# Gated DeltaNet preparation: key norms and write gates move from the VectorE products into the exponent of the decays

## The chip, the cores and the metric

The kernel runs on one core of a Trainium2 chip. The metric is device time in microseconds (us) of one execution. TensorE (PE in the rows) multiplies matrices, VectorE (DVE) and GpSimd (POOL) do elementwise work, ScalarE (ACT) does activations, and DMA queues are fed from SP, ACT and POOL.

## The reference, cut to what matters

One layer of a hybrid block over 256 context and 1024 latent tokens. Four of its heads are a bidirectional gated DeltaNet. For every chunk of tokens and both directions it needs

```
q = l2_normalize(q) * HEAD_DIM ** -0.5;  k = l2_normalize(k)
decay = where(i >= j, exp(G[i] - G[j]), 0)          # G: cumulative log-decay of the chunk
kb = k * beta
A  = where(i > j, (kb @ k.T) * decay, 0)            # then (A + I) is inverted
qk = (q @ k.T) * decay
```

The kernel keeps raw keys and queries in DRAM and puts their norms in later. With `nk` the squared norm of key j (plus epsilon), a column of the matrix and of the scores needs the factor beta/nk beside the decay. The rest of the layer is retention in four more heads, an output projection and a SwiGLU.

## The kernel before

The chunk is 128 tokens, so there are TT = 10 tiles of tokens (tiles 0 and 1 are context), and every tile has two directions d: 20 units. Projections for keys and queries (`conv_block`, with a short convolution on VectorE at L586) and token-major projections (`token_major`, PE tile `tm`) surround the preparation `pre(t)` (L660 to L702). A library scheduler with a timing model sets each engine's order inside one program; TensorE work of later stages is put between the small steps. Each engine then runs its own list strictly in order.

`pre(t)` does for one tile:

- PE: `kk` (L665, keys by keys), for latent tiles also `qt` (L670, transposes whose squares ACT sums at L672) and `kq` (L675). These and the transposes `vT` of the values share three PSUM banks ("pb").
- per direction: `gw` is a broadcast row of G fetched by DMA (L678). POOL subtracts the column's own G with four 128-wide instructions, one a head (L683, `e<-gw,nG`), and masks with one 512-wide affine select (L685). ACT takes the exponential, 512 wide (L687). VectorE multiplies `kk` by the column factor `ab` = beta/nk and by `e`, four 128-wide instructions (L695, into `ut`); for latent tiles it does the same with `kq` (L697, into `sp`). ACT also takes exp of `gw` in place (L700), and POOL multiplies it by the query tile (L701). DMAs take `ut` and `sp` to DRAM.

The tiles `gw`, `e`, `ut` and `sp` have two buffers each. `BATCH` groups the tiles in three sets; after a set, `invert(b)` (L708) does a 62-instruction chain on VectorE, its results go to DRAM as `xd`, and `merge(b)` (L756) fetches them back as `U` and `t` and multiplies 32-wide blocks on PE (tile `m`, L771 to L798). `ab` is made in `kstat` (L609), where it is also a factor of `kds`. `nG` is -G (L553), and `softplus` (L141) gives the log-decays from `av`.

Of the kernel before, what the change touches and what calls it, by code (L numbers as in the profile page):

```python
# [8 lines left out]
F32 = mybir.dt.float32  # L9
F32R = mybir.dt.float32r  # L10
I32 = mybir.dt.int32
AF = mybir.ActivationFunctionType
ALU = mybir.AluOpType
# [4 lines left out]
P = 128  # L18
# [5 lines left out]
TT = NTOK // P  # L24
LT = NLAT // P
H = 4
# [3 lines left out]
NEG = -200.0  # L30
GROUPS = ["rv", "rk", "rq", "rg", "z"]
# [6 lines left out]
def build(nc, tc, ap, dbg=None, stop=None, marks=None):  # L38
    root = ExitStack()
    V, S, G, T, SY = nc.vector, nc.scalar, nc.gpsimd, nc.tensor, nc.sync  # L40
# [30 lines left out]
    def bc(a, shape, axis):  # L71
        return a.unsqueeze(axis).to_broadcast(shape)
# [68 lines left out]
    def softplus(pl, x, n, tag):  # L141

        a = pl.tile([P, n], F32, tag=tag + "a", name=tag + "a")
        s = pl.tile([P, n], F32, tag=tag + "s", name=tag + "s")
        q = pl.tile([P, n], F32, tag=tag + "q", name=tag + "q")
# [12 lines left out]
        return s  # L158

    banks(pa=3, pb=3, pc=2)  # L160
    try:
# [35 lines left out]
        xts, raws, small = {}, {}, {}  # L197
# [327 lines left out]
        def c8(t, d):  # L525
# [6 lines left out]
        av = AB.tile([P, TT * 8], F32, tag="av", name="av")  # L532
        V.tensor_tensor(av.rearrange("p (t c) -> p t c", c=8), xa[:, :, 0:8],
                        bc(small["dtb"], [P, TT, 8], 1), ALU.add)
        S.activation(nA, small["alog"], AF.Exp)
        V.tensor_scalar(nA, nA, -1.0, None, ALU.mult)
        sp = softplus(AB, av, TT * 8, "sp")
# [95 lines left out]
        nkf = nk.rearrange("p t h -> p (t h)")  # L633
        sv = rsqrt(GS, nkf, TT * H, "sv")
# [25 lines left out]
        def pre(t):  # L660
# [15 lines left out]
            for d in range(2):  # L676
# [3 lines left out]
                e = GP.tile([P, H, P], F32, tag="e", name="e", bufs=2)  # L680
                for h in range(H):
                    col = t * 8 + d * 4 + h
                    G.tensor_scalar(e[:, h, :], gw[:, h, :], sm["nG"][:, col:col + 1], 1.0, ALU.add, ALU.mult)  # L683
                sg = 1 if d == 0 else -1
                G.affine_select(out=e, in_=e, compare_op=ALU.is_ge, fill=NEG, base=0,  # L685
                                pattern=[[0, H], [sg, P]], channel_multiplier=-sg)
                S.activation(e, e, AF.Exp)  # L687
# [3 lines left out]
                for h in range(H):  # L691
                    col = t * 8 + d * 4 + h
                    hs = slice(h * P, (h + 1) * P)
                    abc_ = sm["ab"][:, col:col + 1]
                    V.scalar_tensor_tensor(ut[:, h, :], pk[:, hs], abc_, e[:, h, :], ALU.mult, ALU.mult)  # L695
                    if t >= 2:
                        V.scalar_tensor_tensor(sp[:, 0, h, :], pq[:, hs], abc_, e[:, h, :], ALU.mult, ALU.mult)  # L697
# [917 lines left out]
```

## Time and profile before

| | us |
|---|---|
| median of 3 timed runs | 1484.18 (1483.59 to 1484.78) |
| profiled execution, its own time | 1486.29 |
| its span, first to last instruction | 1484.5 |
| TensorE busy in the span | 1406.9 (95%) |
| VectorE / ScalarE / GpSimd busy | 974.2 / 604.9 / 628.4 |
| mean granted TensorE clock, of full speed | 0.977 |

TensorE is busy in nearly all of the span, so the places to look at are those where it is not, or where it runs at the lower clock. The preparation lies between 281 and 372 us; the last two of the ten tiles follow up to 436 us, and the three merges lie between 423 and 537 us.

### The profile page before, as it was taken

What the parts mean: (1) busy time and instruction counts of PE and PEld (TensorE: products, weight loads), DVE (VectorE), ACT (ScalarE), POOL (GpSimd) and SP (SyncE); (2) the same over time, 40 slices, a digit from 0 to 9 for tenths busy, and PEclk for the clock granted to TensorE, in tenths of its full rate; (3) what the DMA queues carried; (4) which work ended last, traced back from release to release, by engine and by line L of the source; (5) the groups of instructions that cost most, each with busy time, mean ns of one, the idle gap of its engine ahead of it and who ended that gap; (6) DMA issues with size and microseconds to landing.
All of it is one profiled execution on the core that took longest, in us unless ns stands there. A gap on an engine that the chain in (4) does not pass through costs nothing.

```text
span 1484.5 us, 24226 instructions
## 1 busy us (share of the span) xinstructions
PE 1406.9 (95%) x8919; PEld 1206.4 (81%) x8919; DVE 974.2 (66%) x1938; ACT 604.9 (41%) x1268; POOL 628.4 (42%) x581
## 2 busy tenths in 40 slices
PE   7999999987988899999799899999999999999997
PEld 2798888976878899999688688777888888788886
DVE  6566788269868345689767876656555555657486
ACT  5543564375541121245534533323333333444454
POOL 0120011377124343234134689899555553335321
PEclk9999999998999899999899999999999999999999
DMA  8536686578597755996633265765222242776863
GB/s 321 208 99 212 188 250 202 165 233 273 175 266 204 248 186 205 414 361 221 204 114 114 85 207 215 258 243 183 106 107 107 106 144 79 237 278 190 308 204 114
DMA packets 176567, 298.16 MB, mean 201 GB/s; under 512 B 43496, under 2 KB 93880, under 8 KB 172096
## 3 DMA queue, kind: packets, MB, share of 16 engines
q1 hardware_dynamic: 124896, 253.17, 49.5%
q10 hardware_dynamic: 49072, 35.83, 7.7%
q0 software_dynamic: 2480, 7.60, 1.4%
q8 instruction: 70, 1.15, 0.3%
q14 instruction: 49, 0.40, 0.1%
HBM read 206.60 MB, written 89.96 MB: 200 GB/s over the span
## 4 chain that ended last, share of the span: by engine, by line
PE 42%; POOL 4%; DMA 2%; DVE 1%; issue 1%; ACT 0%; SPq 0%; POOLq 0%; ACTq 0%; DVEq 0%
PE ffn L1306 7%; PE ffn L1305 7%; PE ffn L1304 7%; PE fo L1432 4%; PE fo L1430 4%; PE fo L1431 4%; PE op L1163 2%; PE op L1164 2%; PE op L1165 2%; DMA wd<-tw 1%; POOL ws L1277 1%; POOL tw L1358 1%; POOL tw L1357 1%; DVE wlo L315 1%; POOL tw L1359 0%
## 5 line engine op out<-in xcount | busy, mean ns | idle before, releaser
L341 PE MATMUL tm<-whi,hhi 128*128 128x256 f32 (+1 forms) x704 | 201.1, 289 | 5.6 <-ACT xa L354 1.6
L342 PE MATMUL tm<-wlo,hhi 128*128 128x256 f32 (+1 forms) x704 | 201.3, 288 | 0.6 <-DVE wlo L315 0.6
L343 PE MATMUL tm<-whi,hlo 128*128 128x256 f32 (+1 forms) x704 | 199.2, 287 | 0.0
L341 PEld LDWEIGHTS tm<-whi,hhi 128*128 128x128 f32 x704 | 134.0, 191 | 10.0 <-ACT xa L354 2.4
L1304 PE MATMUL ffn<-t,whi 128*128 128x512 f32 x352 | 137.0, 390 | 2.0 <-ACT whi L314 2.0
L1306 PE MATMUL ffn<-t,wlo 128*128 128x512 f32 x352 | 137.1, 390 | 1.5 <-DVE wlo L315 1.5
L1305 PE MATMUL ffn<-t,whi 128*128 128x512 f32 x352 | 137.0, 389 | 0.0
L314 ACT ACTIVATE whi<-wraw 128x512 fp32r<-128x512 f32 (+2 forms) x98 | 75.2, 771 | 151.4 <-PE ffn L1305 80.5
L342 PEld LDWEIGHTS tm<-wlo,hhi 128*128 128x128 f32 x704 | 134.6, 191 | 1.8 <-DVE wlo L315 1.1
L343 PEld LDWEIGHTS tm<-whi,hlo 128*128 128x128 f32 x704 | 134.1, 192 | 1.8 <-issue 0.9
L314 ACT ACTIVATE whi<-ws 128x512 fp32r<-128x512 f32 x88 | 55.6, 632 | 175.4 <-PE ffn L1305 121.6
L315 DVE TENSOR_TENSOR wlo<-ws,whi 128x512 fp32r<-128x512 f32 x88 | 94.3, 1073 | 47.7 <-ACT whi L314 47.5
L1430 PE MATMUL fo<-whi,ahi 128*128 128x512 f32 x308 | 119.3, 390 | 1.3 <-ACT ahi L314 1.3
L1431 PE MATMUL fo<-wlo,ahi 128*128 128x512 f32 x308 | 119.9, 389 | 0.0
L1432 PE MATMUL fo<-whi,alo 128*128 128x512 f32 x308 | 119.0, 390 | 0.0
L315 DVE TENSOR_TENSOR wlo<-wraw,whi 128x512 fp32r<-128x512 f32 (+2 forms) x92 | 100.3, 1092 | 25.0 <-ACT whi L314 25.0
L1304 PE MATMUL ffn<-b,whi 128*128 128x512 f32 x264 | 103.9, 393 | 4.1 <-ACT whi L314 4.1
L1306 PE MATMUL ffn<-b,wlo 128*128 128x512 f32 x264 | 103.9, 394 | 1.1 <-DVE wlo L315 1.1
L1305 PE MATMUL ffn<-b,whi 128*128 128x512 f32 x264 | 103.8, 393 | 0.0
L576 PE MATMUL b<-hhi,whi 128*128 128x512 f32 (+1 forms) x256 | 96.3, 376 | 1.5 <-ACT y L580 1.5
L578 PE MATMUL b<-hhi,wlo 128*128 128x512 f32 (+1 forms) x256 | 95.2, 372 | 0.0
L577 PE MATMUL b<-hlo,whi 128*128 128x512 f32 (+1 forms) x256 | 94.9, 371 | 0.0
(427 smaller groups left out, 3494.6 us busy)
## 6 DMA issues: line engine op xcount, KB each, us to landing
adaw<-ada_w SPq DMA_DIRECT2D x48, 512.0 KB, 4.6
pk<-sd SPq DMA_DIRECT2D x16, 1536.0 KB, 10.1
wraw<-wfi SPq DMA_DIRECT2D x44, 512.0 KB, 4.0
ar<-ad SPq DMA_DIRECT2D x33, 512.0 KB, 4.7
w<-wfo SPq DMA_DIRECT2D x22, 512.0 KB, 4.6
wd<-tw SPq DMA_DIRECT2D x11, 1024.0 KB, 4.8
ad<-act SPq DMA_DIRECT2D x20, 512.0 KB, 3.0
raw<-wd SPq DMA_DIRECT2D x20, 512.0 KB, 4.9
```

The costliest lines, as they stand in the source:

```text
L314: S.activation(hi, raw, AF.Copy)
L315: e.tensor_tensor(lo, raw, hi.bitcast(F32), ALU.subtract)
L341: T.matmul(o, hhi[:, k, tsl], whi[:, k % 4, :], start=(k == 0), stop=False)
L342: T.matmul(o, hhi[:, k, tsl], wlo[:, k % 4, :], start=False, stop=False)
L343: T.matmul(o, hlo[:, k, tsl], whi[:, k % 4, :], start=False, stop=(k == KT - 1))
L576: T.matmul(o, whi[:, k, :], hh, start=(k == 0), stop=False)
L1304: T.matmul(o, whi[:, k, :], xhi(xn, slice(0, 4), k), start=(first and k == 0), stop=False, **kw)
L1305: T.matmul(o, whi[:, k, :], xlo(xn, slice(0, 4), k), start=False, stop=False, **kw)
L1306: T.matmul(o, wlo[:, k, :], xhi(xn, slice(0, 4), k), start=False, stop=(k == 3), **kw)
L1430: T.matmul(po[g][i], ahi[:, ts], whi, start=(j == 0 and not kw), stop=False, **kw)
L1431: T.matmul(po[g][i], ahi[:, ts], wlo, start=False, stop=False, **kw)
L1432: T.matmul(po[g][i], alo[:, ts], whi, start=False, stop=(j == FH - 1), **kw)
```

## The change

- `softplus` now runs on two halves at once: the decay's argument and minus the gate's argument, so that its second half is -log(beta). `lnb` is the negated second half.
- A new function `log` takes log(nk) for all 40 columns by exponent and mantissa, 22 VectorE instructions; two more put log(beta) - log(nk) into `nG`.
- In `pre(t)` the four POOL subtractions are gone; the affine select reads `gw` and writes `e`, with -1e30 outside the mask. The exponential becomes four 128-wide ACT instructions, one a head, each with its column of `nG` as bias. The four `ut` products become one 512-wide product of `kk` and `e`, and likewise the `sp` products.

```diff
-        sp = softplus(AB, av, TT * 8, "sp")
+        sp = softplus(AB, av.rearrange("p a n -> p (a n)"), 2 * TT * 8, "sp")
+        lnb = GS.tile([P, TT, 2, H], F32, tag="lnb", name="lnb")
+        V.tensor_scalar(lnb.rearrange("p t d h -> p (t d h)"), sp[:, TT * 8:], -1.0, None, ALU.mult)
+        sp = sp[:, :TT * 8]
...
+        lnk = log(GS, nkf, TT * H, "ln").rearrange("p (t h) -> p t h", h=H)
+        nG4 = sm["nG"].rearrange("p (t d h) -> p t d h", d=2, h=H)
+        V.tensor_tensor(lnb, lnb, bc(lnk, [P, TT, 2, H], 2), ALU.subtract)
+        V.tensor_tensor(nG4, nG4, lnb, ALU.add)
...
                 e = GP.tile([P, H, P], F32, tag="e", name="e", bufs=2)
+                sg = 1 if d == 0 else -1
+                G.affine_select(out=e, in_=gw, compare_op=ALU.is_ge, fill=FAR, base=0,
+                                pattern=[[0, H], [sg, P]], channel_multiplier=-sg)
                 for h in range(H):
                     col = t * 8 + d * 4 + h
-                    G.tensor_scalar(e[:, h, :], gw[:, h, :], sm["nG"][:, col:col + 1], 1.0, ALU.add, ALU.mult)
-                sg = 1 if d == 0 else -1
-                G.affine_select(out=e, in_=e, compare_op=ALU.is_ge, fill=NEG, base=0,
-                                pattern=[[0, H], [sg, P]], channel_multiplier=-sg)
-                S.activation(e, e, AF.Exp)
+                    S.activation(e[:, h, :], e[:, h, :], AF.Exp, bias=sm["nG"][:, col:col + 1])
...
-                for h in range(H):
-                    col = t * 8 + d * 4 + h
-                    hs = slice(h * P, (h + 1) * P)
-                    abc_ = sm["ab"][:, col:col + 1]
-                    V.scalar_tensor_tensor(ut[:, h, :], pk[:, hs], abc_, e[:, h, :], ALU.mult, ALU.mult)
-                    if t >= 2:
-                        V.scalar_tensor_tensor(sp[:, 0, h, :], pq[:, hs], abc_, e[:, h, :], ALU.mult, ALU.mult)
+                V.tensor_tensor(ut.rearrange("p h i -> p (h i)"), pk, e.rearrange("p h i -> p (h i)"), ALU.mult)
+                if t >= 2:
+                    V.tensor_tensor(sp[:, 0].rearrange("p h i -> p (h i)"), pq, e.rearrange("p h i -> p (h i)"), ALU.mult)
```

The scheduler's order changes between the softplus and the first steps of the scan, and is the same before and after that stretch, apart from line numbers. Lines of the changed kernel are 30 to 35 higher in this part: its exponential of `e` is L726, the `gw` exponential L735, the affine select L722, the two products L730 and L732, the silu of the convolution L624.

On ACT, early in the preparation, around the silu of one convolution block (`u` and `y` are the two copies out of a convolution's PSUM bank), the order before is

```order
L589 ACTIVATE y<-y 128x1280
L579 ACTIVATE u<-b_3767 128x512
L580 ACTIVATE y<-b_3767,cw 128x512
L700 ACT_TABLE_LOAD
L700 ACTIVATE gw<-gw 128x512
L687 ACTIVATE e<-e 128x512
L314 ACTIVATE whi<-wraw 128x8x128
L700 ACTIVATE gw<-gw 128x512
```

and around the same silu after the change

```order
L615 ACTIVATE y<-b_3699,cw 128x512
L624 ACT_TABLE_LOAD
L624 ACTIVATE y<-y 128x1280
L726 ACT_TABLE_LOAD
L726 ACTIVATE e<-e,nG 128x128 x4
L712 ACTIVATE qt,nq<-qt 128x128
L735 ACTIVATE gw<-gw 128x512
L712 ACTIVATE qt,nq<-qt 128x128 x2
L726 ACTIVATE e<-e,nG 128x128 x3
```

A unit has four short exponentials where it had one long one, and its `gw` exponential now stands behind them. ACT has 22 table loads in either program.

On SP, the queue that feeds the first merge (`t` and `U` are fetched for it, `rope` is a table loaded into the space of the value tiles), the order before is

```order
L834 DMA rope<-rope 128x1280
L702 DMA sd<-sp 128x1024
L752 DMA t_4269<-xd_3091 32x32x32 x2
L702 DMA sd<-sp 128x1024
L678 DMA gw<-grow_d 128x512
L752 DMA t_4269<-xd_3091 32x32x32 x2
L751 DMA U_4267<-xd_3091 32x32x32 x2
L698 DMA un_2862<-ut 128x512
L751 DMA U_4267<-xd_3091 32x32x32 x2
```

and after the change

```order
L737 DMA sd<-sp 128x1024 x2
L718 DMA gw<-grow_d 128x512
L869 DMA rope<-rope 128x1280
L787 DMA t_4173<-xd_3079 32x32x32 x4
L733 DMA un_2894<-ut 128x512
L786 DMA U_4171<-xd_3079 32x32x32 x4
```

The fetches of `t` stand together directly behind the `rope` load; the store of `sp` and the `gw` fetch that stood between them stand ahead of it.

## Rows read from the trace of the kernel before

**Rows 1.** Stretches: length; busy PE, PEld, DVE, ACT, POOL; clock; DMA share; GB/s

```profile
281.00:372.00 91.00, 77.50 (x428) 66.89 (x426) 71.24 (x177) 55.80 (x124) 65.14 (x94) 0.89 0.73 236
372.00:500.00 128.00, 109.48 (x1545) 105.49 (x1546) 92.95 (x240) 45.02 (x99) 34.23 (x55) 0.93 0.75 218
860.00:950.00 90.00, 90.00 (x399) 74.53 (x398) 62.89 (x63) 25.94 (x44) 81.23 (x53) 1.00 0.63 224
```

**Rows 2.** PE's waits, 281 to 372 us: us in total, times, longest

```profile
PE vT L820 <- DVE ut L695: 3.4, 1, 3.4
PE kk L665 <- ACT qt L672: 3.3, 1, 3.3
PE qt L670 <- DVE ut L695: 3.0, 1, 3.0
PE b L576 <- ACT y L580: 1.5, 3, 0.9
PE vT L820 <- ACT qt L672: 1.1, 1, 1.1
```

**Rows 3.** ACT's waits in the same stretch

```profile
ACT gw L700 <- POOL e L683: 20.9, 8, 5.9
ACT e L687 <- POOL e L685: 4.1, 5, 1.4
```

**Rows 4.** Stretches of 5 us in it, columns as in Rows 1

```profile
330.00:335.00 5.00, 5.00 (x29) 5.00 (x29) 3.88 (x11) 4.64 (x11) 3.23 (x6) 0.60 1.00 373
360.00:365.00 5.00, 4.36 (x14) 3.27 (x15) 4.33 (x11) 3.12 (x8) 3.21 (x5) 0.50 0.95 296
```

**Rows 5.** Groups by line, 281 to 372 us: busy us, mean ns, idle before

```profile
L695 DVE SCALAR_TENSOR_TENSOR ut<-kk,ab,e 128x128 f32<-128x128 f32 x64 | 19.1, 341 | 32.1 <-ACT e L687 32.1
L697 DVE SCALAR_TENSOR_TENSOR sp<-kq,ab,e 128x128 f32<-128x128 f32 x48 | 14.6, 340 | 0.0
L683 POOL TENSOR_SCALAR e<-gw,nG 128x128 f32<-128x128 f32 x64 | 31.9, 515 | 23.0 <-DVE ut L695 15.9 <-DVE tmp L730 3.8 <-DMA gw<-grow_d 1.7
L687 ACT ACTIVATE e<-e 128x512 f32<-128x512 f32 x18 | 11.1, 626 | 4.3 <-POOL e L685 4.1
```

**Rows 6.** Single lines and a timeline row: nearest forms of the new instructions

```profile
L977 ACT ACTIVATE XI<-dist,lgs x8: 388/391/393, 608.7 to 610.7; 128x128 f32<-128x128 f32 x8
L1036 DVE TENSOR_TENSOR pm<-rP,M x8: 661/682/699, 643.7 to 714.9; 128x512 f32<-128x512 f32 x8
360.71 1.14 ACT L823 ACTIVATE vt<-vT,svy 128x128 f32<-128x128 f32 x4 [3.03 <-DMA sd<-vt]
L113 DVE TENSOR_TENSOR svu<-svy x3: 192/192/199, 230.4 to 235.9; 128x40 f32<-128x40 f32 x3
```

**Rows 7.** ACT's timeline: start us, us, instruction, idle before it

```profile
323.48 0.63 ACT L700 ACTIVATE gw<-gw 128x512 f32<-128x512 f32 x1 [1.88 <-POOL e L683]
325.22 1.28 ACT L589 ACT_TABLE_LOAD   x1
327.69 0.26 ACT L672 ACTIVATE qt<-qt 128x128 f32<-128x128 f32 x1
```

**Rows 8.** PE's waits, 415 to 500 us, and SP's timeline there

```profile
PE m L778 <- DMA U<-xd: 4.0, 2, 3.0
PE m L771 <- DMA t<-xd: 3.9, 3, 2.6
...
419.15 3.41 SPq L702 DMA_DIRECT2D sd<-sp  x1
423.09 1.63 SPq L752 DMA_DIRECT2D t<-xd  x2
```

**Rows 9.** PE's timeline: two token-major matmuls in a row

```profile
254.80 0.28 PE L341 MATMUL tm<-whi,hhi 128*128 128x256 f32 x1
254.92 0.28 PE L342 MATMUL tm<-wlo,hhi 128*128 128x256 f32 x1
```

**Rows 10.** VectorE's timeline: the first product of the preparation

```profile
283.16 2.16 DVE L695 SCALAR_TENSOR_TENSOR ut<-kk,ab,e 128x128 f32<-128x128 f32 x8 [23.70 <-ACT e L687]
```

More of the change, by code (lines that the diff above doesn't have):

```diff
@@ L30 @@
 NEG = -200.0
+FAR = -1e30
 GROUPS = ["rv", "rk", "rq", "rg", "z"]
@@ L158, in softplus, with log @@
         return s
+    def log(pl, x, n, tag):
+        i = pl.tile([P, n], I32, tag=tag + "i", name=tag + "i")
+        m = pl.tile([P, n], F32, tag=tag + "m", name=tag + "m")
+        e = pl.tile([P, n], F32, tag=tag + "e", name=tag + "e")
+        f = pl.tile([P, n], F32, tag=tag + "f", name=tag + "f")
+        V.tensor_scalar(i, x.bitcast(I32), 23, None, ALU.logical_shift_right)
+        V.tensor_copy(e, i)
+        V.tensor_scalar(m.bitcast(I32), x.bitcast(I32), 0x7FFFFF, 0x3F800000, ALU.bitwise_and, ALU.bitwise_or)
+        V.tensor_scalar(f, m, 1.4142135, None, ALU.is_gt)
+        V.scalar_tensor_tensor(e, e, -127.0, f, ALU.add, ALU.add)
+        V.tensor_scalar(f, f, -0.5, 1.0, ALU.mult, ALU.add)
+        V.tensor_tensor(m, m, f, ALU.mult)
+        V.tensor_scalar(f, m, 1.0, None, ALU.add)
+        V.reciprocal(f, f)
+        V.scalar_tensor_tensor(f, m, -1.0, f, ALU.add, ALU.mult)
+        q = m
+        V.tensor_tensor(q, f, f, ALU.mult)
+        a = pl.tile([P, n], F32, tag=tag + "a", name=tag + "a")
+        V.tensor_scalar(a, q, 1.0 / 15.0, None, ALU.mult)
+        for k in (13, 11, 9, 7, 5, 3):
+            V.scalar_tensor_tensor(a, a, 1.0 / k, q, ALU.add, ALU.mult)
+        V.scalar_tensor_tensor(a, a, 1.0, f, ALU.add, ALU.mult)
+        V.tensor_scalar(f, e, 0.6931471805599453 - 0.693359375, None, ALU.mult)
+        V.scalar_tensor_tensor(a, a, 2.0, f, ALU.mult, ALU.add)
+        V.scalar_tensor_tensor(a, e, 0.693359375, a, ALU.mult, ALU.add)
+        return a
     banks(pa=3, pb=3, pc=2)
@@ L531, in build @@
         CHUNKS = [(0, 256), (256, 512), (768, 512)]
-        av = AB.tile([P, TT * 8], F32, tag="av", name="av")
-        V.tensor_tensor(av.rearrange("p (t c) -> p t c", c=8), xa[:, :, 0:8],
-                        bc(small["dtb"], [P, TT, 8], 1), ALU.add)
+        av = AB.tile([P, 2, TT * 8], F32, tag="av", name="av")
+        av3 = av.rearrange("p a (t c) -> p a t c", c=8)
+        V.tensor_tensor(av3[:, 0], xa[:, :, 0:8], bc(small["dtb"], [P, TT, 8], 1), ALU.add)
+        V.tensor_scalar(av3[:, 1], xa[:, :, 8:16], -1.0, None, ALU.mult)
         S.activation(nA, small["alog"], AF.Exp)
         V.tensor_scalar(nA, nA, -1.0, None, ALU.mult)
-        sp = softplus(AB, av, TT * 8, "sp")
+        sp = softplus(AB, av.rearrange("p a n -> p (a n)"), 2 * TT * 8, "sp")
+        lnb = GS.tile([P, TT, 2, H], F32, tag="lnb", name="lnb")
+        V.tensor_scalar(lnb.rearrange("p t d h -> p (t d h)"), sp[:, TT * 8:], -1.0, None, ALU.mult)
+        sp = sp[:, :TT * 8]
         V.tensor_tensor(sm["g"].rearrange("p (t c) -> p t c", c=8), sp.rearrange("p (t c) -> p t c", c=8),
```

## The prediction

> **What bounds the kernel now.** I read the busy time by stretch first. In the feed-forward part TensorE is busy in all of the 90 us shown and runs at full clock [rows 1]: nothing that the change touches can be worth anything there, and the order of instructions there is unchanged. In the preparation, 281 to 372 us, TensorE is busy for only 77.5 of 91 us, and its granted clock is 0.89 [rows 1]. So 13.5 us are idle. The clock adds to that: a granted 0.60 in a stretch of 5 us with TensorE fully busy costs 2.0 us, and 0.50 with 4.36 us busy costs 2.2 us [rows 4]. (1 - 0.89) x 91 = 10.0 us is the most that the low clock can cost in the stage; part of it falls on idle time, and I put 7 us on work. The stage thus loses about 20.5 us. From 372 to 500 us another 18.5 us are idle at a clock of 0.93 [rows 1]; this is where the merges are.
>
> Then I read TensorE's waits in that stage, because they say which engine would have to be earlier. VectorE's `ut` products release PSUM banks late, for 3.4 + 3.0 = 6.4 us; ACT is late for 3.3 us and 1.1 us with the squares of `qt`, and for 1.5 us with the convolution's copies, 5.9 us together [rows 2]. Both engines have a cause further back. VectorE waits for the exponential of `e` for 32.1 us in the stage [rows 5], of which 23.7 us stand ahead of its first product and cost nothing [rows 10], so 8.4 us inside. ACT, busy for 55.8 of 91 us [rows 1], waits for POOL: its in-place exponential of `gw` must wait until POOL's four subtractions have read `gw`, 20.9 us in 8 waits, and 4.1 us for the affine select [rows 3]. POOL's subtractions hold 31.9 us of its time in the stage, 64 at a mean of 515 ns [rows 5]. The loop is therefore POOL to ACT to VectorE to the PSUM bank to TensorE, and POOL's subtractions are its longest member.
>
> **The change, part by part.** *POOL.* The 64 subtractions in the stage go, 31.9 us of 65.1 us busy [rows 1, 5]. What stays is the affine select. ACT's wait of 20.9 us was for the removed instruction; what is late next for the `gw` exponential is the affine select, for which ACT waited 4.1 us in all [rows 3].
>
> *VectorE.* The stage's 64 + 48 products, 19.1 + 14.6 = 33.7 us [rows 5], become 16 + 12 = 28 products, 512 wide, with one operand in PSUM. The nearest row has the same form: 0.682 us [rows 6]. That is 28 x 0.682 = 19.1 us, a saving of 14.6 us of VectorE's 71.2 us in the stage [rows 1].
>
> *ACT.* Of 18 exponentials in the stage at 0.626 us [rows 5] each becomes four. No row has an exponential with a per-partition bias. The nearest are eight 128-wide exponentials with a per-partition scale, started within 2.0 us and 0.39 us long, so 1.2 us for four, and a packet of four scaled copies at 1.14 us [rows 6]. I take 1.2 us, since that is the same function on SBUF. The addition is 18 x (1.2 - 0.626) = 10.3 us; ACT then needs 55.8 + 10.3 = 66.1 us in a stage in which TensorE's work at full clock is 77.5 - 7 = 70.5 us. A rule speaks against the change here: the Trainium skill, "ScalarE: Activation LUTs", in the section on what ACT_TABLE_LOAD costs, gives an activation with a pointer bias a fixed part of about 280 ns, of which about 93 ns overlap with a neighbour. By that rule, as an estimate, four would take 1.27 us and the addition in the stage would be 11.6 us, close to the rows' price; no row shows the bias form itself.
>
> *Logarithm and gate.* 24 small VectorE instructions at 0.19 us, from a 40-wide row [rows 6], are 4.6 us, plus some 2 us for the doubled softplus by the same row. They lie ahead of 283 us, where VectorE idles for 23.7 us before its first product [rows 10]. I cost them at nothing; without that cover they would delay the first exponentials by at most 6.6 us, and TensorE has convolution work there.
>
> *What leaves TensorE's path.* The `ut` waits, 6.4 us [rows 2]: the products are shorter, their input comes earlier; I take all of it off. The clock: the low stretches lie in the part of the stage in which TensorE waits, so with fewer waits I take off 5 of the 7 us (bounds 0 and 7). The waits for ACT, 5.9 us: the order of squares, table loads and silu on ACT is of the same kind as before. The wait of 3.3 us for `qt` came from a 1.88 us wait for POOL followed by a table load and a silu between two squares [rows 7]; the first part goes, but four exponentials stand among the squares now. I leave all of it standing. Bounds: it goes (-5.9), or ACT's additional 10.3 us comes on top (+10.3). A value nearer to the first bound is right because up to 25.0 us of ACT's waits for POOL [rows 3] fall away against 10.3 us of added work.
>
> *Merges.* In the first merge TensorE waits 3.9 us for `t` [rows 8]. SP had spent 3.41 us on a store of `sp` ahead of the second pair of fetches, issued at 423.09 us [rows 8]; now the four fetches follow the `rope` load directly. I take 2 us off; bounds 0 and -3.9. Between the first merge's last product and the next one's second stage there were 128 + 38 token-major matmuls and are 115 + 34 + 3, 14 fewer at 0.12 us [rows 9]: the wait of 4.0 us for `U` [rows 8], at the end of a chain of stores and fetches with a length of its own, grows by 1.7 us.
>
> The sum: -6.4 - 5 - 2 + 1.7 = -11.7 us. From the profiled execution's 1486.3 us that is 1474.6 us; the median of the runs shown is 2.1 us lower, so I say 1472.5, rounded to 1473 us.
>
> **The rivals.** *More than that.* If ACT's late squares were all POOL's doing, the stage would lose only a few us: -20.5, with -3.9 and +1.7 in the merges, -22.7 us, 1461.5 us. For it: the waits for POOL are the largest in the stage [rows 3]. Against: ACT would be busy for 66.1 of about 71 us, in order, with waits on TensorE itself.
>
> *The gain is given back (no change).* The stage ends earlier, but the merges hang on a chain of VectorE's inversion, stores and fetches, and the values' copies, which have one buffer and wait for the store of the one before (3.03 us in one instance [rows 6]). If the stage's 11.4 us only become waits at the first merge, the sum is 0 to -3: 1481 to 1484 us. Against: TensorE has token-major work to put there, and the inversion on VectorE speeds up with the rest.
>
> *ACT becomes the bound (slower).* ACT serves the squares, the convolution's copies and the value copies for which TensorE already waits. If ACT's waits for POOL turn into waits for something else of the same length (VectorE's release of `e`, or `gw`'s fetch), the 10.3 us pass through to TensorE, while the 6.4 us of `ut` waits, which follow ACT, stay: 1484.2 + 10.3 = 1494.5 us. ACT is idle for 91 - 55.8 = 35.2 us of the stage [rows 1]; at an unchanged length the added work leaves 24.9 us. So this case begins where ACT's waits after the change come to more than 24.9 us in the stage. A milder form, with half of it, gives 1489 us.
>
> *The change doesn't do what it says*, by more table loads: ACT has 22 in either program, so I give that no chance of its own.
>
> **How the numbers follow.** A measurement here can tell 0.2%, 3 us, from no change. Forecast, -5 to -17 us: 0.60; more: 0.14; given back: 0.16; slower by ACT: 0.10. Of the forecast's own range all lies beyond -3 us, of the given-back case nearly all within. Faster 0.74, same 0.16, slower 0.10. The forecast's range is 1467 to 1479; down to 1462 takes in most of the first rival, and up to 1485 the second; the third is left out.
>
> **What would show it.** The preparation should take 78 to 82 us instead of 91, with TensorE's waits on the `ut` product nearly gone and its waits on `qt` and on the convolution's copies still there. ACT's wait for POOL should fall from 25 us to under 8, POOL's busy time in the stage to about 33 us. The products should cost 0.66 to 0.70 us, four exponentials 1.1 to 1.3 us. The first merge should wait less for `t`, the second somewhat more for `U`. After the merges all stretches should have their old lengths. I am wrong if ACT is busy to over 90% of a stage that did not shorten, or if the first merge waits longer by what the stage gained.

## The result, and the profile after

The changed kernel takes 1489.57 us, median of 16 runs (1485.42 to 1496.22), against 1484.86 us before: a ratio of 1.0032, 95% interval 1.0020 to 1.0043. It is 0.3% slower; 1473 us was forecast, with 1485 as the upper end. Repeated on another chip it took 1490.54 us, ratio 1.0039 (1.0025 to 1.0053). The first profile is of the fastest of its 16 runs (1485.42 us, span 1483.3 us) and so shows less than the whole loss. The second, of the repetition, is of an execution of 1490.93 us, span 1488.8 us, close to its median. Both are used below, and a reading is kept where they agree.

The single operations became what was forecast. Groups by line after the change, 281 to 372 us (line, engine, operation, tiles, shapes, count, busy us, mean ns, then idle before them and what ended it):

```profile
L730 DVE TENSOR_TENSOR ut<-kk,e 128x512 f32<-128x512 f32 x16 | 10.9, 687 | 36.0 <-PE kk L705 22.1 <-ACT e L726 8.4 <-POOL e L722 3.4
L732 DVE TENSOR_TENSOR sp<-kq,e 128x512 f32<-128x512 f32 x12 | 8.1, 678 | 0.0
L726 ACT ACTIVATE e<-e,nG 128x128 f32<-128x128 f32 x72 | 23.1, 390 | 16.8 <-POOL e L722 16.3 <-ACT vt L858 0.5
L722 POOL TENSOR_SCALAR_AFFINE_SELECT e<-gw 128x512 f32<-128x512 f32 x16 | 13.8, 865 | 32.7 <-DMA gw<-grow_d 14.8 <-DVE ut L730 13.4 <-DVE y L621 4.2
```

VectorE's 112 products of 33.7 us [rows 5] are 28 of 19.0 us, the 64 subtractions on POOL are gone, and the exponentials cost 23.1 us where they cost 11.1.

The stages show where it goes wrong. Stretches of the kernel before, from 372 us, and of the first profile after, from 281 us (length; busy PE, PEld, DVE, ACT, POOL; granted clock; DMA share; GB/s):

```profile
372.00:420.00 48.00, 44.98 (x377) 44.24 (x378) 36.43 (x88) 24.87 (x70) 7.36 (x9) 1.00 0.66 196
420.00:500.00 80.00, 64.50 (x1170) 61.24 (x1169) 56.52 (x154) 20.15 (x30) 26.86 (x46) 0.89 0.80 232
500.00:540.00 40.00, 40.00 (x589) 38.57 (x588) 13.44 (x39) 8.70 (x16) 18.32 (x35) 1.00 0.59 193
```

```profile
281.00:372.00 91.00, 77.78 (x445) 68.36 (x444) 70.39 (x104) 68.06 (x180) 34.74 (x30) 0.91 0.77 238
372.00:420.00 48.00, 40.39 (x330) 39.78 (x329) 32.54 (x75) 21.43 (x65) 4.89 (x5) 0.93 0.70 214
420.00:500.00 80.00, 68.63 (x1202) 65.37 (x1201) 53.19 (x131) 22.88 (x38) 26.19 (x43) 0.89 0.73 199
500.00:540.00 40.00, 38.23 (x571) 36.72 (x569) 13.47 (x38) 6.62 (x12) 15.97 (x31) 1.00 0.66 224
```

In the preparation TensorE issues more matmuls than before in the same 91 us (445 against 428 [rows 1]), at a clock of 0.91 instead of 0.89. In the next 48 us it loses them: 7.6 us idle instead of 3.0, 330 matmuls instead of 377, and a clock of 0.93 instead of 1.00. From 420 to 540 us, where the merges are, it idles for 13.1 us instead of 15.5 (12.8 in the second profile). From 281 to 540 us that makes 32.0 us of idle time before, and 34.0 and 35.5 after.

The same in milestones. First and last start of the convolution's matmuls (b) and of the token-major matmuls (tm), which fill TensorE's gaps until the merges are over; before, then after the change in the second profile:

```profile
L576 PE MATMUL b<-hhi,whi x256: 276/392/796, 112.0 to 370.5; 128*128 128x512 f32 x96, 128*128 128x256 f32 x32
L341 PE MATMUL tm<-whi,hhi x704: 274/281/582, 38.2 to 581.2; 128*128 128x256 f32 x157, 128*128 128x272 f32 x19
```

```profile
L611 PE MATMUL b<-hhi,whi x256: 276/392/796, 112.0 to 366.9; 128*128 128x512 f32 x96, 128*128 128x256 f32 x32
L371 PE MATMUL tm<-whi,hhi x704: 274/281/582, 38.8 to 586.2; 128*128 128x256 f32 x157, 128*128 128x272 f32 x19
```

The convolution ends 3.6 us earlier (365.7 us, 4.8 earlier, in the first profile), and the last tm starts 5.0 us later (583.5, 2.3 later). The execution of the second profile is 4.6 us longer than that of before (1490.93 against 1486.29): the whole loss is there when the filler ends, and nothing after it adds to it. In all 20 profiles of this study 900 to 907 us lie between the last tm's start and the end of the execution. That spread is as wide as the loss, so a single profile's last tm says only roughly what a kernel's median will be.

### The profile page after: what moved, and what is told of

The parts are those of the page before. It is cut to its first block, busy times and chain, and to the rows that moved or that the text cites. A ratio compares the mean times of both kernels' runs of the same rounds, so it can differ in the third digit from the quotient of the medians.

```text
span 1483.3 us, 24109 instructions
## 1 busy us (share of the span) xinstructions
PE 1404.5 (95%) x8919; PEld 1205.9 (81%) x8919; DVE 974.3 (66%) x1856; ACT 616.4 (42%) x1328; POOL 591.8 (40%) x501
## 4 chain that ended last, share of the span: by engine, by line
PE 39%; POOL 6%; DMA 2%; issue 1%; DVE 1%; ACT 1%; POOLq 0%; ACTq 0%; DVEq 0%
PE ffn L1341 7%; PE ffn L1339 6%; PE ffn L1340 6%; PE fo L1465 4%; PE fo L1467 4%; PE fo L1466 4%; PE op L1198 2%; PE op L1200 2%; PE op L1199 2%; DMA wd<-tw 2%; POOL ws L1312 1%; POOL tw L1393 1%; POOL tw L1392 1%; POOL tw L1395 1%; POOL tw L1394 1%
```

## Where the preparation's gain is lost

ScalarE copies the convolution's values, up to four token tiles of one head at a time, out of PSUM into `vt`, which has one buffer, and stores it. The next copy waits for that store. Shortly after, SyncE's queue issues the first merge's 2048-KB fetch of `U`. ScalarE's timeline before, 402 to 408 us (start us, us, instruction, in brackets the idle time before it and what ended it), and then SyncE's:

```profile
402.14 1.14 ACT L823 ACTIVATE vt<-vT,svy 128x128 f32<-128x128 f32 x4 [2.79 <-DMA sd<-vt]
403.32 0.43 ACTq L824 DMA_DIRECT2D sd<-vt  x1
406.30 1.14 ACT L823 ACTIVATE vt<-vT,svy 128x128 f32<-128x128 f32 x4 [2.06 <-DMA sd<-vt]
407.46 0.37 ACTq L824 DMA_DIRECT2D sd<-vt  x1
```

```profile
405.07 0.48 SPq L747 DMA_DIRECT2D U<-un  x1
415.95 0.33 SPq L834 DMA_DIRECT2D rope<-rope  x1
```

The same two after the change, first profile, and then TensorE's longest wait from 372 us on:

```profile
400.95 1.14 ACT L858 ACTIVATE vt<-vT,svy 128x128 f32<-128x128 f32 x4 [1.52 <-DMA sd<-vt]
402.12 0.37 ACTq L859 DMA_DIRECT2D sd<-vt  x1
411.30 1.14 ACT L858 ACTIVATE vt<-vT,svy 128x128 f32<-128x128 f32 x4 [8.93 <-DMA sd<-vt]
412.46 0.37 ACTq L859 DMA_DIRECT2D sd<-vt  x1
```

```profile
401.83 0.39 SPq L782 DMA_DIRECT2D U<-un  x1
417.97 0.33 SPq L869 DMA_DIRECT2D rope<-rope  x1
```

```profile
PE kk L705 <- ACT vt L858: 6.8, 1, 6.8
```

Before, the fetch (405.07) had only the last store behind it (407.46), and no copy waited for that one. With the shorter preparation the fetch starts at 401.83, 0.3 us ahead of the store of 402.12, so two stores stand behind it. That store lands at about 411 us, 9 us after its issue. The copy waits 8.93 us for `vt`, the PSUM bank that it was to empty stays taken, and TensorE stands at `kk` for 6.8 us. It is in order, so the filler that could run stands behind. The second profile has the same: fetch at 403.27, store at 403.78, next copy at 412.87 after 8.85 us, `kk` waiting 6.7 us. The `rope` load, which waits for stores of ScalarE's queue, comes 2 us later than before (417.97 against 415.95), and the first two blocks of the merge's `t` behind it 1.5 us later (418.40 against 416.86), though the preparation ended earlier.

Stretches of 4 us after the change show the collision and its second price:

```profile
404.00:408.00 4.00, 1.70 (x15) 1.50 (x14) 3.26 (x7) 0.00 (x0) 0.63 (x1) 1.00 0.94 317
408.00:412.00 4.00, 0.00 (x0) 0.00 (x0) 1.85 (x5) 0.70 (x3) 0.00 (x0) 0.66 0.68 257
412.00:416.00 4.00, 3.51 (x16) 3.51 (x17) 0.00 (x0) 2.27 (x12) 0.00 (x0) 0.50 0.95 328
```

The DMA engines are 94% busy while TensorE runs dry. Having idled, TensorE then works from 412 us at a granted 0.50, the lower of its two levels, so 3.51 us of busy time there do the work of 1.8.

## The experiments

Ratios are to the kernel before, timed beside each kernel on the same chip; "fetch" is the first `U<-un`. The expectations name theories. *ACT*: the four exponentials' extra time passes through ScalarE to TensorE. *Loop*: the preparation is held by something else, gw's two buffers above all. *Order*: the new logarithm instructions shift the scheduler's order, and that is the loss. *Downstream*, sharpened to *collision* after the first four kernels: the gain is made and lost after 372 us.

| kernel | median us | ratio (95%) | fetch, us | values' stores issued after it | last tm, us | profiled execution, us |
|---|---|---|---|---|---|---|
| before | 1484.86 | 1 | 405.1 | 1 (the last) | 581.2 | 1486.3 |
| after | 1489.57 | 1.0032 (1.0020–1.0043) | 401.8 | 2 | 583.5 | 1485.4 |
| after, again | 1490.54 | 1.0039 (1.0025–1.0053) | 403.3 | 2 | 586.2 | 1490.9 |
| before, exponential split | 1483.48 | 0.9994 (0.9976–1.0011) | 403.9 | 1 | 581.0 | 1481.5 |
| before, logarithms unused | 1485.65 | 1.0001 (0.9985–1.0018) | 405.0 | 1 | 581.4 | 1485.0 |
| products alone | 1487.90 | 1.0019 (1.0002–1.0036) | 401.9 | 2 | 583.7 | 1486.1 |
| bias alone | 1487.96 | 1.0010 (0.9996–1.0024) | 401.9 | 1 | 585.1 | 1491.5 |
| after, 3 gw | 1486.59 | 1.0011 (0.9997–1.0025) | 399.3 | 2 | 583.2 | 1487.5 |
| after, fetch behind the stores | 1483.09 | 0.9987 (0.9975–0.9998) | 408.8 | 0 | 581.4 | 1485.0 |
| before, fetch behind the stores | 1485.41 | 0.9999 (0.9987–1.0011) | 409.9 | 0 | 582.2 | 1484.6 |
| after, 2 vt | 1482.57 | 0.9988 (0.9978–0.9999) | 392.3 | 0 | 581.2 | 1481.5 |
| before, 2 vt | 1487.47 | 1.0010 (1.0001–1.0018) | 393.4 | 0 | 585.9 | 1488.1 |
| after, 2 vt, 3 gw | 1486.46 | 1.0006 (0.9993–1.0019) | 387.3 | 0 | 579.8 | 1484.6 |
| after, gw first | 1486.98 | 1.0006 (0.9991–1.0020) | 401.3 | 1 | 578.1 | 1482.2 |
| after, gw first, 2 vt | 1481.98, 1482.47 | 0.9971 (0.9961–0.9981), 0.9979 (0.9966–0.9992) | 386.0, 385.2 | 0 | 574.3, 574.3 | 1481.6, 1477.5 |
| products alone, 2 vt | 1483.83 | 0.9997 (0.9981–1.0013) | 389.9 | 0 | 582.5 | 1482.3 |
| bias alone, 2 vt | 1479.20, 1479.96 | 0.9956 (0.9939–0.9973), 0.9964 (0.9950–0.9978) | 387.0, 388.5 | 0 | 576.2, 583.1 | 1476.0, 1488.4 |
| bias alone, gw first, 2 vt | 1490.44 | 1.0036 (1.0019–1.0053) | 386.8 | 1 (the last) | 590.8 | 1495.2 |

The two profiles of the bias alone with two `vt` buffers differ by 6.9 us at the last tm. A single profile thus can't place two or three us, and sizes below are taken from the ratios.

**First: which part.** The products alone on the changed kernel:

```diff
-                G.affine_select(out=e, in_=gw, compare_op=ALU.is_ge, fill=FAR, base=0,
-                                pattern=[[0, H], [sg, P]], channel_multiplier=-sg)
                 for h in range(H):
                     col = t * 8 + d * 4 + h
-                    S.activation(e[:, h, :], e[:, h, :], AF.Exp, bias=sm["nG"][:, col:col + 1])
+                    G.tensor_scalar(e[:, h, :], gw[:, h, :], sm["nG"][:, col:col + 1], 1.0, ALU.add, ALU.mult)
+                G.affine_select(out=e, in_=e, compare_op=ALU.is_ge, fill=NEG, base=0,
+                                pattern=[[0, H], [sg, P]], channel_multiplier=-sg)
+                S.activation(e, e, AF.Exp)
```

> The products' part alone: the logarithms go into nG and VectorE takes 28 wide products in the stage, but POOL keeps its four subtractions a unit and ACT its one 512-wide exponential. Theory ACT (the four short exponentials, some 11 us more on ScalarE's list, ate the gain): faster than before by 5 to 8 us, about 1478 us. Theory loop (the fetch, mask, exponential, product of gw in two buffers became the bound since the gw exponential stands behind four exponentials): the loop is as before here, so also faster, by 3 to 8 us. Theory order (the scheduler's new order alone moves the time by some us, whatever the instructions cost): anything within 5 us of before. Theory downstream (the preparation ends earlier but the values' copies and the merges wait as long): within 3 us of before, with the convolutions ending 5 us earlier.

The kernel before with its exponential of `e` in four instructions:

```diff
-                S.activation(e, e, AF.Exp)
+                for h in range(H):
+                    S.activation(e[:, h, :], e[:, h, :], AF.Exp)
```

> Before, with only the exponential of e split into four 128-wide ones; POOL's subtractions and all VectorE products stay. Theory ACT: 18 x 0.65 us = 11 us more on ScalarE in the stage, and since it waits for POOL for 25 us there, part is hidden; slower than before by 4 to 10 us, 1489 to 1495 us. Theory loop: the gw exponential is released by POOL's subtractions and need not stand behind the others, so the time is within 3 us of before, 1482 to 1488 us.

The kernel before with the logarithm computed and used by nothing:

```diff
+            lnk = log(GS, nkf, TT * H, "ln")
```

> Before, with the 22 VectorE instructions of the logarithm added and their result not used. They cost 4.3 us of VectorE ahead of the preparation, where it idles. Theories ACT, loop and downstream: within 2 us of before. Theory order: the scheduler places other work differently and the time moves by 3 us or more, either way.

And the changed kernel with a third buffer for gw:

```diff
-                gw = GP.tile([P, H, P], F32, tag="gw", name="gw", bufs=2)
+                gw = GP.tile([P, H, P], F32, tag="gw", name="gw", bufs=3)
```

> The changed kernel with a third buffer for gw (room made by one tag for the inversions' scratch tiles, which run one after the other). Theory loop: POOL's waits for the gw fetch fall from 14.8 us in the stage to under 5 us and the time falls by 5 to 10 us against the changed kernel, to 1480 to 1485 us. Theory ACT: POOL waits less for the fetch, but ScalarE's list is as long; no change, 1487 to 1492 us. Theory downstream: the convolutions end earlier, the end does not move.

The logarithms alone and their shift of the order are worth nothing (1.0001): *order* falls. The split exponential costs no time either, but it was a weaker test than I meant. Its row, of the same stretch:

```profile
L688 ACT ACTIVATE e<-e 128x128 f32<-128x128 f32 x72 | 16.2, 300 | 0.6 <-POOL e L685 0.2
```

A 128-wide exponential without a bias is 300 ns, so ScalarE got 16.2 - 11.1 = 5 us more to do and not 10. The third gw took away much of what held the loop (ScalarE's wait for POOL's select fell from 16.3 to 7.0 us, and the convolution ended at 362.9 us), and yet this kernel is no faster than the one before, and about 0.2% under the changed one: little of what is gained ahead of 372 us reaches the end. TensorE waits there at `kk` for `vt` as well, 7.3 us in two waits. The products alone show the collision at its clearest: store issued at 401.87, fetch at 401.86, the copy waits 11.60 us, `kk` 10.2 us. They have neither the four exponentials nor the changed loop, both *ACT* and *loop* had them faster by 3 to 8 us, and they came out 0.2% slower.

**Second: is it the collision.** Two buffers for `vt` in the changed kernel, and the same edit in the kernel before:

```diff
-                vt = CV.tile([P, 4, P], F32, tag="vt", name="vt", bufs=1)
+                vt = CV.tile([P, 4, P], F32, tag="vt", name="vt", bufs=2)
```

> The changed kernel with two buffers in place of one for the values' scaled copies (vt), nothing else; the scheduler moves some transposes of the values ahead. Collision (my theory now: the 2048-KB fetch U<-un starts at 401.8 instead of 405.1, the store of a values' copy issued at 402.1 lands 9 us later, and the one buffer vt holds ScalarE, and TensorE behind its PSUM banks, until then): TensorE's 6.8 us of kk on vt go to under 2, ScalarE's 8.9 us before vt to under 3; the last kk ends at about 408 as before the change, the third merge at 533 to 537 instead of 539.9, and the time is 4 to 7 us under the changed kernel's, about 1483. Merges (rival: the merges hang on VectorE's inversion of the last units and on the blocks' fetches, whatever the values do): the wait goes, the last merge ends within 1 us of 539.9, time within 1.5 us of the changed kernel. Front (rival: the gain before 372 was never one): the time as the changed kernel, and the last kk at 411 or later.

> The kernel before with two buffers for vt. Collision: there the fetch U<-un begins when only one store of the values is left, so the buffer costs at most the 2 to 3 us waits on each store that ScalarE shows, which TensorE mostly does not share: 0 to 2 us faster, 1483 to 1485. Merges: within 1 us of before. A rival that the second buffer is worth the same everywhere (it is not the collision): 4 to 6 us faster, 1479 to 1481.

And, with one `vt` still, the fetch issued on ScalarE's queue behind the last store; later the same in the kernel before:

```diff
-            SY.dma_start(uu.rearrange("p e c h j -> p e (c h) j"), un[b])
+            with tc.issue_after(last_vt[0]) if b == 0 else nullcontext():
+                (S if b == 0 else SY).dma_start(uu.rearrange("p e c h j -> p e (c h) j"), un[b])
...
-                S.dma_start(vd[t0:t0 + n, :, h, :].rearrange("t p j -> p t j"), vt[:, :n])
+                last_vt[0] = S.dma_start(vd[t0:t0 + n, :, h, :].rearrange("t p j -> p t j"), vt[:, :n]).ins
```

> The changed kernel with the first fetch U<-un issued on ScalarE's queue behind the last store of the values, and not on SyncE's: one buffer vt still. Collision: the store of 402 lands in 3 to 4 us again, ScalarE's wait falls from 8.9 to about 3, TensorE's kk on vt from 6.8 to under 2, the last kk ends near 407; the fetch U lands at about 416 and the first merge's products of U start no later than now; 3 to 6 us under the changed kernel, 1484 to 1486. If instead the stores are slow for another reason (sd<-sp, rows of un), the wait stays over 6 us. Merges: wait gone, time within 1.5 us of the changed kernel or up to 3 us over it, since U is late.

> The kernel before with the first fetch U<-un issued on ScalarE's queue behind the last store of the values. Collision: before the change the fetch starts at 405.1, and the only store it can delay is the last (407.5), on which no copy waits any more, so the move gives 0 to 1 us, 1484 to 1486, and TensorE's idle time from 372 to 420 stays at about 3 us. A rival that the move is worth its 0.45% in any kernel: 5 to 7 us faster, 1478 to 1481.

ScalarE's timeline in the changed kernel with the fetch behind the stores, and TensorE's share of 372 to 420 us there:

```profile
406.12 1.14 ACT L860 ACTIVATE vt<-vT,svy 128x128 f32<-128x128 f32 x4 [2.15 <-DMA sd<-vt]
407.30 0.37 ACTq L861 DMA_DIRECT2D sd<-vt  x1
408.75 1.78 ACTq L783 DMA_DIRECT2D U<-un  x1
```

```profile
372.00:420.00 48.00, 45.40 (x380) 44.32 (x380) 37.38 (x90) 25.11 (x71) 4.79 (x5) 1.00 0.66 202
```

The store that had taken 9 us lands in 2.4 us (403.73 to 406.12), the wait of `kk` is gone, TensorE is idle for 2.6 us of the stretch instead of 7.6, and its clock is 1.00 again. The time falls from a ratio of 1.0032 to 0.9987, 0.45% or 6.7 us. That this is near the 6.8 us of the wait is in part chance: TensorE's idle time from 281 to 540 us is 34.2 us in this profile, hardly less than in the changed kernel's two (34.0 and 35.5), since other waits come in its place (3.4 us for the fetch of `U`, 2.2 us for `pk`). What is better is the clock: 0.94 up to 372 us and 1.00 from there to 420, against 0.91 or 0.92, and 0.93.

In the kernel before, where no copy waits on a store behind the fetch, the same move gives nothing (0.9999). It lets `rope` start earlier in both kernels (411.79 against 417.97 in the changed one, 410.97 against 415.95 in the one before), so that isn't what the changed kernel gains by. An edit that takes away the collision is thus worth 0.45% in the kernel that has it and nothing in the one that hasn't: the collision is shown to be the cause, and it is worth more than the whole loss. The two ratios' intervals don't meet (1.0020 to 1.0043, 0.9975 to 0.9998). How the time comes back, by which waits and how much by the clock, isn't settled by one profile.

Two buffers for `vt` agree with this (0.9988 in the changed kernel, 1.0010 in the one before), but they are the weaker test. What they are worth does not follow the length of the wait at `kk`: 0.2% in the products alone, which wait there for 10.2 us, and 0.5% in the bias alone, which doesn't wait there at all (both below).

It is not so that earlier merges are a gain in themselves. With two `vt` buffers the third merge's last product starts at 521.4 us instead of 539.9, 18.5 us earlier, of which 7 us reach the end; the kernel before with two `vt` has it 10.7 us earlier (525.7 against 536.4) and is 0.1% slower. In that kernel other waits come instead: TensorE's filler waits for ScalarE (`res`) for 10.7 us from 372 to 420 us, where the kernel with one `vt` has no such wait, and TensorE's idle time from 372 to 500 us is 21.3 us instead of 18.5. It is moved, not saved.

Two `vt` and three gw together:

> The changed kernel with two buffers for vt and three for gw, the work area that the row fetch, the exponentials and VectorE's products pass on (room made by letting the forward and the backward work area tmp share one name). Collision, with the loop's own wait for gw gone too (three gw alone ended the convolution 2.8 us earlier, 362.9, and gave 1486.6): convolution's end about 362, last kk near 405, third merge at 531 to 535, time 1479 to 1482, under both kernels. Merges: convolution's end 362, but the last merge at 538 to 540 and 1485 to 1488.

Again earlier merges (third merge's last product at 517.0 us) and no gain, which speaks against *loop* as well, and against my sum of the two.

**Third: what the change is worth once the collision is off.** The bias alone keeps VectorE's products at 128 columns:

```diff
-                V.tensor_tensor(ut.rearrange("p h i -> p (h i)"), pk, e.rearrange("p h i -> p (h i)"), ALU.mult)
-                if t >= 2:
-                    V.tensor_tensor(sp[:, 0].rearrange("p h i -> p (h i)"), pq, e.rearrange("p h i -> p (h i)"), ALU.mult)
+                for h in range(H):
+                    hs = slice(h * P, (h + 1) * P)
+                    V.tensor_tensor(ut[:, h, :], pk[:, hs], e[:, h, :], ALU.mult)
+                    if t >= 2:
+                        V.tensor_tensor(sp[:, 0, h, :], pq[:, hs], e[:, h, :], ALU.mult)
```

> The changed kernel with VectorE's eight products by 128 columns, as before the change, in place of two by 512: the bias alone. Sum of the parts: the products alone gave 1487.9, so the loss is in what both have in common, VectorE's ut and the fetch U earlier. If the bias alone also brings the fetch U<-un ahead of two stores (start under 403.5), kk waits on vt and it is 1487 to 1490; if its slower products keep the fetch at 404 or later, no wait on vt over 3 us and 1483 to 1486. Front theory (the exponentials' own cost is the loss): 1488 to 1492 whatever the fetch does.

> The changed kernel as it is, on the chip of this call, for a second profile and a direct comparison with the two that follow. Collision: TensorE's wait of kk on vt is there again, 5 to 12 us, with U<-un at 400 to 403 while two stores of the values are out, and TensorE's filler (the last tm) ends 2 to 3 us later than in the kernel before, 583 to 585; median 1488 to 1491, ratio to before 1.002 to 1.004. Chance (rival: the 0.3% was the draw of one chip, the first profile, at 1485.4, showing the truth): median 1484 to 1486 and kk without a wait on vt in the new profile.

> The products alone (512-wide products and logarithms in the column factor, GpSimd's subtractions and the one 512-wide exponential as before the change) with two buffers for vt. Collision: alone with one buffer it was 1.0019 with an 11.6 us wait of vt on its store; with two the wait goes, and it is 3 to 6 us faster than that: ratio to before 0.998 to 1.000, 1482.5 to 1486. If the loss were in the products themselves it stays at 1.001 to 1.003.

> The bias alone (four biased exponentials, GpSimd's subtractions gone, VectorE's products by 128 columns) with two buffers for vt. Alone with one buffer it had no kk wait on vt, ended the convolution 2.6 us earlier than the changed kernel, and lost it again in the merges (TensorE idle 16.1 us from 420 to 500 and 4.4 from 500 to 540), 1.0010. Collision in the wide sense (the fetch and the stores delay the first merge's blocks too): the merges come 10 to 18 us earlier as they did with two buffers elsewhere, TensorE's idle from 281 to 585 falls from 35 to 30 to 32 us, ratio 0.998 to 1.000. If the bias itself is the loss: 1.001 or more again.

> The bias alone with two vt buffers, once more. My theory: a product of 128 columns starts after its own exponential (0.39 us) and one of 512 only after all four (1.28), so ut, its store and TensorE's bank come later by up to 0.9 us a pair with 512, more than VectorE's 7.7 us of busy time saved are worth, since VectorE is not what is waited for; ratio 0.995 to 0.997, under both parts with two vt buffers (0.9988, interval to 0.9978). If the first result was the draw of six runs: 0.998 to 0.9995, as both parts.

The changed kernel again, on another chip, shows the wait of `kk` (6.7 us) and the loss (1.0039) once more, so neither was chance. With two `vt` everywhere, and so without the collision: neither part 1.0010, products 0.9997, bias 0.9956 and 0.9964, both 0.9988. The bias is worth 0.5%, the four exponentials' full price included: ScalarE is busy for 73.1 us of 91 in the stage there, more than in the changed kernel, and this is the fastest kernel of the study. That rules out *ACT* as the cause of the loss. The wide products on top of it take 0.2 to 0.3% away; without the bias they cost nothing (0.9997 against 1.0010). VectorE's rows of the narrow products with the bias:

```profile
L732 DVE TENSOR_TENSOR ut<-kk,e 128x128 f32<-128x128 f32 x64 | 15.5, 281 | 30.1 <-ACT e L726 28.9 <-ACT y L615 1.2
L734 DVE TENSOR_TENSOR sp<-kq,e 128x128 f32<-128x128 f32 x48 | 11.3, 278 | 0.0
```

They are busy for 26.8 us instead of 19.0, but of the 30.1 us of waiting 22.0 are the first, so 8.1 lie inside the stage, against 36.0 - 22.1 = 13.9 for the wide ones. I had expected a reason in the exponentials: a narrow product can start after the first one, 0.39 us, and a wide one only after four, 1.28 us. The products alone speak against it. Their `e` comes from a single 512-wide exponential, and their wide products wait inside the stage for just as long, 35.9 - 22.0 = 13.9 us:

```profile
L731 DVE TENSOR_TENSOR ut<-kk,e 128x512 f32<-128x512 f32 x16 | 10.8, 685 | 35.9 <-PE kk L705 22.0 <-ACT e L727 13.9
```

So VectorE's waits go with the width of the products and not with the number of exponentials: what it no longer works, it mostly waits (26.8 + 8.1 = 34.9 us narrow, 19.0 + 13.9 = 32.9 wide). Why the narrow products make the faster kernel beside the bias is open.

The bias alone with one `vt` (1.0010) has no `kk` wait on `vt`, though its fetch starts at 401.9 us and a wait was expected for that; only the last store stands behind the fetch, and it still gains nothing; TensorE idles for 16.1 us from 420 to 500 us and 4.4 from 500 to 540 there. What the second buffer removes in that case is open.

ScalarE's exponential of gw ahead of the four biased ones:

```diff
+                if t >= 2:
+                    S.activation(gw, gw, AF.Exp)
                 for h in range(H):
                     col = t * 8 + d * 4 + h
...
-                    S.activation(gw, gw, AF.Exp)
```

> The changed kernel with the query's exponential of gw ahead of the four biased ones, one buffer for vt. The front gains a further 2 to 4 us (convolution's end 362 to 364). If the collision stands (U<-un with two stores of the values out), kk waits on vt for 5 us or more, and it is 1486 to 1491, at best 1.000; if the best kernel's gain was the order of the exponentials alone, 1480 to 1483 here too. If the new order happens to leave one store only behind the fetch: no wait, and 1483 to 1486.

> The changed kernel with two buffers for vt and with the query's exponential of gw ahead of the four biased ones on ScalarE's program. TensorE's idle total (my theory: what counts is TensorE's unoccupied time and its clock from 281 us to the end of its filler at 581, 30.4 us idle with two vt against 34.0 without): GpSimd's product no longer waits for the four exponentials, ScalarE's wait for the select shrinks from 15.6 to under 8, TensorE's vT on qt (6.4) falls; idle 27 to 30 us, the last tm at 578 to 581, 1479 to 1482.5. If the merges or the scan set the end instead, 1482 to 1484 as with two vt alone. Against it: VectorE's ut waits for the exponentials that now come later, up to 1.1 us of 20 pairs, and 1484 to 1487.

> The best kernel so far once more (two vt buffers, the query's exponential first). It repeats: ratio to before 0.996 to 0.998, 1480 to 1483. If the first 0.9971 was the draw of a chip: 0.9985 or more.

> The bias alone with two vt buffers and the query's exponential ahead of the four. Beside 512-wide products that order gave 0.1 to 0.2%; here it holds back the first 128-wide product by the 0.62 us of the query's exponential, and VectorE shows most of its waits on e. Order worth the same: 0.993 to 0.995, 1475 to 1478. Order and narrow products in each other's way: 0.9955 to 0.998.

With one `vt`, a store issued at 401.01 still meets the fetch of 401.26: the copy waits 6.12 us, `kk` 3.7, ratio 1.0006. With two it is 0.9971 and 0.9979, 0.1 to 0.2% under two `vt` alone (0.9988), with intervals that overlap. Beside the narrow products I expected 0.993 to 0.998 and got 1.0036. Its timeline (ScalarE's, then SyncE's) and SyncE's longest wait there:

```profile
386.88 0.41 ACTq L862 DMA_DIRECT2D sd<-vt  x1
```

```profile
386.82 0.38 SPq L785 DMA_DIRECT2D U<-un  x1
397.62 0.33 SPq L872 DMA_DIRECT2D rope<-rope  x1
398.52 2.16 SPq L790 DMA_DIRECT2D t<-xd  x2
```

```profile
SPq L872 <- DMA sd<-vt: 10.2, 2, 8.6
```

Here the last store is issued 0.06 us after the fetch, and `rope`, which waits for it, comes at 397.62 with the merge's `t` at 398.52. Without the reordering the last store was 2.5 us ahead of the fetch (384.53 and 386.99) and `t` came at 389.87. So the collision is back in another place. But the convolution ends 3 us later too (365.9 us, 362.9 and 363.1 without the reordering), ahead of any fetch of the merge. Which of the two makes the 0.7 to 0.8% wasn't tried apart.

## Why the prediction was wrong

- **POOL, right.** Busy for 34.7 us of the stage; about 33 was said.
- **The products, right in price, wrong in worth.** 28 x 0.682 = 19.1 us was forecast and 19.0 measured. That narrower ones would serve TensorE better was not considered.
- **The exponentials, right.** Four take 1.28 us, 1.2 by the nearest row [rows 6] and 1.1 to 1.3 as the sign to look for; the addition is 23.1 - 11.1 = 12.0 us instead of 10.3. The estimate from the Trainium skill, "ScalarE: Activation LUTs" (what ACT_TABLE_LOAD costs), 1.27 us and 11.6, was the nearer one: the trace agrees with it, and the bias form is 90 ns longer than the exponential without bias (390 against 300 ns).
- **ACT's wait for POOL, wrong.** Under 8 us was said; it is 16.3 in 7. The row of `e` shows why: the select waits 14.8 us for gw's row fetch. Before, POOL's first instruction of a pair waited 1.7 us for that fetch [rows 5].
- **The waits on `ut`, right and worth less.** They are gone. TensorE's waits in the first profile, 281 to 372 us:

```profile
PE vT L855 <- ACT qt L712: 5.9, 1, 5.9
PE kk L705 <- issue: 3.0, 2, 2.4
PE b L611 <- ACT y L615: 1.9, 1, 1.9
PE tm L371 <- ACT whi L344: 1.3, 1, 1.3
```

  The named waits of [rows 2] add to 12.3 us, these with two small ones to 12.9. The term of -6.4 us assumed that TensorE, let go by VectorE, would wait for nothing else; it waits for ScalarE's squares instead (5.9 us, before 4.4), and at `kk` for 3.0 us with no releaser in the profile.
- **The clock, mis-sized.** -5 us was said. From 0.89 to 0.91 and 0.92 in the two profiles is 0.02 to 0.03 x 91 = 1.8 to 2.7 us.
- **So the preparation** gained 3.6 to 4.8 us, by the convolution's end, and not 11.4; TensorE idles for 13.2 and 14.9 us of its 91, before 13.5. That is the first failed step, and alone it would still have left a small gain: 0.9988 is what the changed kernel gives once the collision is off.
- **Between the preparation and the merges, the step that turned the sign.** The sum has no term for this stretch: a longer wait of the values' copies is put at nothing, as if stores and fetches kept their order and lengths. The runs showed 6.8 us of waiting at `kk`, 7.6 us of idle time from 372 to 420 us instead of 3.0, and a clock of 0.93 instead of 1.00. The two terms for the merges themselves are not what failed. At the merges' products of `t` and `U` TensorE waited 6.1 us (3.9 for `t` [rows 8], 2.2 for the fetch of `U`) and waits 3.1 in the first profile, with no releaser named, though the first of `t` is issued at 418.40 and 420.09 us instead of 416.86. Its named waits for `U<-xd` are 4.0 us as before, without the 1.7 us more. But all of it comes later: the first merge's first product at 432.5 and 434.0 us instead of 423.6, the third merge's last at 539.9 and 542.5 instead of 536.4. The prediction had the link in its hands: "the values' copies, which have one buffer and wait for the store of the one before", at 3.03 us [rows 6]. It stood under the rival *given back*, with a price that could not be more than the gain, and against it that TensorE has token-major work to put there. Both fail at one place: an earlier start of the fetch changed which transfer stands ahead of which, 3 us became 9, and in-order TensorE stood at `kk` with its filler behind. The condition named at the end, "if the first merge waits longer by what the stage gained", nearly describes it; the wait lies ahead of the merge, at `kk`.
- **The rivals.** *ACT becomes the bound* gave the right sign for the wrong reason: its condition, waits of ACT in the stage above 24.9 us, was not met (91 - 68.06 = 22.9 us of idle time in all), and the bias alone with two `vt` buffers refutes it. That its milder form gives 1489 us, the time that was measured, is luck.

## What to carry to other kernels

Before a stage is shortened, list the transfers that its end releases and the small stores under way at that moment: a large fetch that moves ahead of a store can cost more than the stage gained, and a one-buffer copy behind that store hands it to every engine. Try a change of this kind together with one more buffer at that place: here the bias alone with two buffers for `vt` takes 1479.2 and 1480.0 us, ratios 0.9956 and 0.9964, faster than both kernels, while neither part of it alone is. It is no sure gain: with two `vt` the kernel before, the changed one with three gw, and the bias alone with gw first lie at 1.0006 to 1.0036. And less busy time on an engine that is seldom waited for need not help: the wide products save VectorE 7.8 us in the stage, and beside the bias the kernel with them is 0.2 to 0.3% slower.

## What the runs showed of the hardware

- A store of 256 KB of values that landed in 2.4 to 2.6 us on a quiet stretch took about 9 us when it was issued 0.3 to 0.5 us after a 2048-KB fetch on another queue, as long as the fetch itself (8.8 and 8.9 us to landing); issued 0.01 us after it, it took 12.5 us. The Trainium skill, "DMA: Bandwidth & Descriptors" (queues, rings and completion order), says that a DMA engine alternates between queues packet by packet. With packets of one size that would about double the store's time, to some 5 us as an estimate from the 2.4 to 2.6; the measurement is above it. The two queues' packets are of very different size, as the first profile after shows from 404 to 409 us, while both transfers are under way (queue, fed by SyncE for q1 and by ScalarE for q10; packets, MB, share of the 16 engines' time):

```profile
q1 hardware_dynamic: 106, 1.74, 97.2%
q10 hardware_dynamic: 41, 0.02, 1.4%
```

  That is some 16 KB a packet of the fetch against 0.5 KB of the stores, which get 1.4% of the engines' time. Whether the engines take strict turns isn't shown by it.
- After a gap of TensorE's (1.70 us busy of 4, then 0.00) the clock granted to the next matmuls was 0.50, the lower of the two levels, where the kernel before, busy for 45.0 of the 48 us, had 1.00 from 372 to 420 us.
- A 128x128 exponential took 300 ns without a bias (the kernel before with the exponential split) and 390 ns with a per-partition one (the changed kernel); a 128x128 product of a PSUM and an SBUF operand 280 ns as a plain product, 341 ns as the three-operand form of before [rows 5].
- Executions of one kernel differ by more than the change is worth: on one chip the bias alone with two `vt` took from 1477.2 to 1488.4 us, and its two profiles (two chips) have spans of 1474.3 and 1486.6 us, more than half of the difference (6.9 us) being there at the last tm. Why is open.
